# RWKV-7 inside a hybrid decoder step: even and odd heads on opposite partition halves, small products alternating between the two

## The chip, the cores and the metric

The kernel runs on one core of one Trainium2 chip. The metric is the device time of one execution in microseconds (us). All arithmetic that matters is in 32-bit floats: the large projections split each operand into two fp32r parts and make three products of them, the small recurrent products use plain f32. In the trace a plain f32 product of two operands appears as two weight loads and two matmul records; a transpose appears as one. Counts of records below are counts in the trace, not of calls in the code.

## The reference, cut to what matters

One layer runs RWKV-7 heads and HGRN2 heads side by side from one input projection, joins them in one output projection, and follows with a squared-ReLU MLP. It does so for a prompt of 1024 tokens and for 8 decode sequences of 4 tokens ("samples"). Only the RWKV part is touched:

```python
def step(s, inp):
    r_t, w_t, k_t, v_t, kk_t, a_t = inp
    sa = jnp.einsum('bhvk,bhk->bhv', s, -kk_t)
    s = (s * w_t[:, :, None, :] + sa[..., None] * (kk_t * a_t)[:, :, None, :]
         + v_t[..., None] * k_t[:, :, None, :])
    o = jnp.einsum('bhvk,bhk->bhv', s, r_t)
    return s, o
```

There are 8 heads of width 64. The kernel doesn't step through tokens. It takes chunks of 64 tokens, builds for each head the 64x64 matrices that say how tokens of the chunk act on each other, inverts one triangular matrix per head, and carries a 64x64 state per head from chunk to chunk.

## The kernel before, in words

The program has two halves. The first, the **mixers**, computes the input projection, the RWKV and HGRN2 recurrences and the conditioning (`ada_pair`); the second does the output projection and the MLP with a Strassen-like scheme (`out_project`, `up`, `down`, products on line 1137) and isn't touched. In the mixers three generators are emitted in turn: the main one (projections `ps_in`, lines 208 to 210, and HGRN2), `ada`, and `rwkv`. Their yields set the order in which work is emitted; a list scheduler then orders each engine's queue at build time, and every engine runs its queue in that order.

RWKV takes the prompt in 8 groups of 128 tokens (2 chunks each) and one group for the samples (1 chunk). A group passes through these stages, and three groups are in flight at a time:

- `rwkv_prep` loads the projected rows as 4 tiles (index j) of 128 partitions. Partitions 0 to 63 of tile j hold one head (h = 0, even), 64 to 127 the next (h = 1, odd). The low-rank products `ps_lora` (line 695) use rows 0 to 63 of a weight for the decay and rows 64 to 127 for the gate `a`. Line 747 and 749 write `bb` and `kd` into the tile `bk`. `ps_v` (line 769) transposes v into token-major form, 4 transposes a group, and line 772 copies it to `R`.
- `rwkv_attn`: `ps_A` (line 793), per chunk and head half 4 products of 64 rows and 128 columns; two VectorE multiplications by a mask (line 795) give `Aa` and `Ar`. Then `ps_bt` (line 809) and `ps_W` (line 815): per chunk 8 products with 64 rows, 64 columns, 64 moving columns. All of one chunk's `ps_W` read one half of the partitions and write the other: which half is set by the chunk's parity, not by the head.
- `rwkv_inv`, on GpSimd, inverts 32x32 blocks that travel through DRAM (`at_d`, `xt_d`); `rwkv_inv2` joins them with three rounds of small products (`ps_x0`, `ps_x1`, `ps_x2`: lines 896, 900, 904), 8 products of 32x32 a round and chunk, each round followed by a copy on ScalarE that the next round needs. One chunk's products all lie at one partition offset.
- `rwkv_chain` carries the state: `ps_U` (line 928) for h = 0, a VectorE add (line 929), `ps_U` for h = 1, another add, `ps_SA` (line 933), a copy (line 934) into `R`, `ps_S` (line 940), the new state (lines 946, 947), and `ps_O` (lines 953 and 954), where for each j and h a 64x64 product of `ar` with the state is followed by a product of `Ar` with `R` over all 128 rows, into the same place. `rwkv_centre` evacuates `ps_O`.
- `rwkv_finish` normalises and writes the output rows.

`ps_S` has a form worth knowing: over all 128 rows, it writes for each j first output partitions 0 to 63 (h = 0), then 64 to 127 (h = 1).

PSUM for RWKV consists of four single-buffered tags, `PT = "maso"`: one bank each for `rwkv_prep` ("m"), `rwkv_attn` and `rwkv_inv2` ("a"), `ps_U`, `ps_SA` and `ps_S` ("s"), and `ps_O` and the output transposes ("o").

Of the kernel before, what the change touches and what calls it, by code (L numbers as in the profile page):

```python
# [7 lines left out]
F32 = mybir.dt.float32  # L8
# [6 lines left out]
P = 128  # L15
# [51 lines left out]
B_Aa = 4  # L67
# [52 lines left out]
LEVELS = [1, 2, 4, 8, 16, 32, 64]  # L120

# [34 lines left out]
class Kernel:  # L156
# [511 lines left out]
    def rwkv_prep(self, g, pool, pp, x_d):  # L668
# [3 lines left out]
        c0, n, nch, sample = g["c0"], g["n"], g["nch"], g["sample"]  # L672
        X = pool.tile([P, 14, n], F32, tag="X", name="X", bufs=B_X)
# [18 lines left out]
        for li, dst, bias in ((slice(0, 64), sg, self.hw0), (slice(64, 128), a, self.ha0)):  # L692
            ps = pp.tile([P, 4, n], F32, tag=PT[0], name="ps_lora")
            for j in range(4):
                nc.tensor.matmul(ps[:, j, :], lhsT=self.lora[li, 0, j * P:(j + 1) * P], rhs=X[li, 12, :], start=True, stop=True)
            for j in range(4):
# [15 lines left out]
        g["bk"] = bk = pool.tile([P, 4, nch, P], F32, tag="bk", name="bk", bufs=B_bk)  # L712
        bx = bk.rearrange("p j c (s t) -> p j (c s) t", t=64)
        bb, kd = bx[:, :, 1:1 + nch, :], bx[:, :, 0::3, :] if nch == 2 else bx[:, :, 0:1, :]
        S.activation(rd, ch(cs), AF.Exp, scale=-DECAY0)
        S.activation(kd, ch(cs), AF.Exp, scale=DECAY0)
        S.activation(al, ch(sg), AF.Exp, scale=-DECAY0)
        g["pt"] = pt = pool.tile([P, 4, NS if sample else nch], F32, tag="pt", name="pt", bufs=B_pt)
# [10 lines left out]
        G.tensor_tensor(ch(a), ch(a), kd, op=ALU.mult)  # L729
# [37 lines left out]
        ps = pp.tile([n, 4, P], F32, tag=PT[0], name="ps_v")  # L767
        for j in range(4):
            nc.tensor.transpose(ps[:, j, :], v[:, j, :], self.ident)
        for e in range(nch):  # L770
            hs = slice(e * 64, (e + 1) * 64)
            S.activation(R[e].rearrange("p j h v -> p (j h v)")[hs, :], ps[hs].rearrange("p j x -> p (j x)"), AF.Copy)
        yield

    def rwkv_attn(self, g, pool, pp):
# [4 lines left out]
        g["Aa"], g["Ar"], g["bt_"] = [], [], []  # L780
        mask = self.amask_s if sample else self.amask
        nhf = 1 if sample else 2
        ni = nch * nhf * 8
# [1085 lines left out]
```

## Time and profile before

| what | us |
|---|---|
| runs shown, median of 3 (lowest to highest) | 1934.76 (1928.95 to 1952.22) |
| the profiled execution, its own time | 1959.38 |
| its span in the trace | 1957.6 |
| TensorE matmul busy | 1793.7 (92% of the span) |
| VectorE / ScalarE / GpSimd busy | 1175.9 / 919.0 / 994.3 |

The profiled execution is 1.3% slower than the median of the runs. A busy matmul engine in these profiles counts each record from start to its modelled end, so neighbours overlap: whether products follow each other densely is read from start to next start in the timeline, or by comparing groups that move the same number of columns. The granted clock is a share of 2.4 GHz; it is either 1 or one half at any moment, so a mean of 0.83 over a stretch means that a third of the stretch ran at 1.2 GHz.

### The profile page before, as it was taken

To read this page: it belongs to the slowest core of one execution; us is meant where nothing else is said; L and a number is where in the kernel's file an instruction comes from. 1 tells how busy PE (TensorE), PEld (TensorE's weight loads), DVE (VectorE), ACT (ScalarE), POOL (GpSimd) and SP (SyncE) were. 2 spreads that over 40 slices of the span, in tenths; PEclk is the share of its full clock that TensorE was granted. 3 is DMA by queue.
4 is the path that set the end of the run, shared out by engine and by line. 5 is a ranking of instruction groups with operands and counts; after the bars stand their busy time and mean duration, and the time that the engine had idled before them with its cause. 6 is when DMAs were issued, how large, how long until landed. Compare 5 with 4: busy or idle time off the path is not lost. (4 is left out here: it accounts for less than half of the span.)

```text
span 1957.6 us, 38042 instructions
## 1 busy us (share of the span) xinstructions
PE 1793.7 (92%) x13988; PEld 1646.0 (84%) x13988; DVE 1175.9 (60%) x2286; ACT 919.0 (47%) x1915; POOL 994.3 (51%) x1418
## 2 busy tenths in 40 slices
PE   6889889899899999999999799699999999999795
PEld 3778778767788888888888799699999899999795
DVE  7676834534744534565544456853333768799998
ACT  5455343653534455555463454545455454333332
POOL 4766362363617233336263566764544637264564
PEclk9998899867679878888796899899999999999896
DMA  7876578645558775635352743353333431423022
GB/s 264 280 235 192 174 237 262 196 125 138 146 154 262 232 230 157 195 117 175 114 160 64 250 170 104 107 167 117 98 99 125 145 132 53 136 75 127 19 76 89
DMA packets 219593, 303.33 MB, mean 155 GB/s; under 512 B 48616, under 2 KB 111464, under 8 KB 216336
## 3 DMA queue, kind: packets, MB, share of 16 engines
q1 hardware_dynamic: 199232, 275.74, 44.6%
q10 hardware_dynamic: 20080, 25.11, 3.8%
q8 instruction: 110, 1.80, 0.4%
q14 instruction: 75, 0.61, 0.1%
q0 software_dynamic: 96, 0.07, 0.0%
HBM read 237.17 MB, written 61.44 MB: 153 GB/s over the span
## 5 line engine op out<-in xcount | busy, mean ns | idle before, releaser
L1137 PE MATMUL ps_g<-bh,whi 128*128 128x264 f32 x1792 | 377.6, 291 | 51.1 <-DVE acc L1449 15.6
L1137 PE MATMUL ps_g<-bh,wlo 128*128 128x264 f32 x1792 | 374.3, 290 | 3.2 <-DVE wlo L1126 3.2
L1137 PE MATMUL ps_g<-bl,whi 128*128 128x264 f32 x1792 | 376.3, 290 | 0.7 <-DVE bl L1426 0.6
L1137 PEld LDWEIGHTS ps_g<-bh,whi 128*128 128x128 f32 x1792 | 287.7, 193 | 55.2 <-ACT whi L1125 16.3
L210 PE MATMUL ps_in<-h,wlo 128*128 128x256 f32 (+1 forms) x960 | 299.0, 313 | 10.0 <-POOL wlo L199 5.6
L208 PE MATMUL ps_in<-h,whi 128*128 128x256 f32 (+1 forms) x960 | 301.1, 318 | 5.7 <-ACT h L1090 3.5
L209 PE MATMUL ps_in<-l,whi 128*128 128x256 f32 (+1 forms) x960 | 298.3, 311 | 3.4 <-DVE l L1091 3.3
L1137 PEld LDWEIGHTS ps_g<-bh,wlo 128*128 128x128 f32 x1792 | 286.0, 193 | 3.8 <-DVE wlo L1126 3.8
L1137 PEld LDWEIGHTS ps_g<-bl,whi 128*128 128x128 f32 x1792 | 287.4, 194 | 1.3 <-DVE bl L1426 1.3
L195 ACT ACTIVATE whi<-wraw 128x512 fp32r<-128x512 f32 x240 | 149.5, 628 | 183.3 <-PE ps_in L209 122.4
L210 PEld LDWEIGHTS ps_in<-h,wlo 128*128 128x128 f32 x960 | 200.1, 209 | 23.1 <-POOL wlo L199 7.9
L208 PEld LDWEIGHTS ps_in<-h,whi 128*128 128x128 f32 x960 | 200.0, 210 | 14.7 <-issue 4.6
L209 PEld LDWEIGHTS ps_in<-l,whi 128*128 128x128 f32 x960 | 200.9, 209 | 10.1 <-DVE l L1091 4.3
L1125 ACT ACTIVATE whi<-wd 128x512 fp32r<-128x512 f32 x112 | 70.1, 630 | 184.2 <-PE ps_g L1137 152.8
L238 POOL TENSOR_TENSOR walo<-wada,wahi 128x256 fp32r<-128x256 f32 x128 | 95.9, 762 | 97.6 <-ACT wahi L237 88.3
L1126 POOL TENSOR_TENSOR wlo<-wu,whi 128x512 fp32r<-128x512 f32 x64 | 90.2, 1412 | 83.4 <-ACT whi L1125 83.2
L1125 ACT ACTIVATE whi<-wu 128x512 fp32r<-128x512 f32 x112 | 69.3, 628 | 119.6 <-PE ps_g L1137 111.0
L1426 POOL TENSOR_TENSOR bl<-u,bh 128x528 fp32r<-128x528 f32 x34 | 63.1, 1862 | 87.9 <-ACT bh L1425 77.8
L862 POOL TENSOR_TENSOR itmp<-ixt,iat 128x60 f32<-128x60 f32 (+24 forms) x248 | 76.1, 307 | 36.0 <-DMA iat<-at_d 17.6
L1426 DVE TENSOR_TENSOR bl<-u,bh 128x528 fp32r<-128x528 f32 x78 | 88.5, 1163 | 5.4 <-ACT bh L1425 5.3
L1126 DVE TENSOR_TENSOR wlo<-wd,whi 128x512 fp32r<-128x512 f32 x91 | 82.7, 913 | 12.3 <-ACT whi L1125 12.3
L864 POOL TENSOR_TENSOR ixt<-ixt,itmp 128x60 f32<-128x60 f32 (+24 forms) x248 | 78.1, 315 | 15.3
(426 smaller groups left out, 3910.7 us busy)
## 6 DMA issues: line engine op xcount, KB each, us to landing
wraw<-w_in SPq DMA_DIRECT2D x240, 256.0 KB, 4.1
wlo<-wlo_d SPq DMA_DIRECT2D x180, 256.0 KB, 3.9
wu<-w_up SPq DMA_DIRECT2D x74, 256.0 KB, 3.0
u<-u_d SPq DMA_DIRECT2D x16, 1056.0 KB, 4.9
wada<-w_ada SPq DMA_DIRECT2D x64, 256.0 KB, 3.8
wd<-w_down SPq DMA_DIRECT2D x64, 256.0 KB, 2.7
wlo_d<-wlo SPq DMA_DIRECT2D x60, 256.0 KB, 3.3
u_d<-c SPq DMA_DIRECT2D x48, 264.0 KB, 3.4
```

The source lines that it names most:

```text
L195: nc.scalar.activation(hi, raw, AF.Copy)
L208: nc.tensor.matmul(out, lhsT=wh, rhs=ah, start=first and k == 0, stop=False)
L209: nc.tensor.matmul(out, lhsT=wh, rhs=al, start=False, stop=False)
L210: nc.tensor.matmul(out, lhsT=wl, rhs=ah, start=False, stop=last and k == len(w) - 1)
L238: (nc.vector if k in ADV else nc.gpsimd).tensor_tensor(lo, raw[:, :, k, :], hi.bitcast(F32), op=ALU.subtract)
L862: G.tensor_tensor(tm, xt[:, 0:ns, j:j + 1].to_broadcast([P, ns, w]), at[:, j, j + 1:32].unsqueeze(1).to_broadcast([P, ns, w]), op=ALU.mult)
L864: G.tensor_tensor(dst, dst, tm, op=ALU.add)
L1125: self.nc.scalar.activation(hi, src, AF.Copy)
L1126: eng.tensor_tensor(lo, src, hi.bitcast(F32), op=ALU.subtract)
L1137: nc.tensor.matmul(out[c], lhsT=w[x][:, k, :], rhs=a[y][:, k, c * 264:c * 264 + 264], start=first and k == 0 and j == 0, stop=last and k = ...
L1426: F().tensor_tensor(lo[:, k, :], src[:, k, :], hi[:, k, :].bitcast(F32), op=ALU.subtract)
```

## The change

The token-side operands are laid out by head parity instead of chunk parity: within `bk`, `Aa`, `W`, `U`, `XT` and `R`, the even heads' part lies on one half of the partitions and the odd heads' on the other, for every chunk. Each group of small products then loops over j outside and the two halves inside, so that consecutive products lie on different partition halves of the operands (and, but for `ps_A` and `ps_lora`, of the output). `ps_lora` and `ps_A` use two PSUM tags ("m" and "a") at a time, one for each half. `ps_O` is split: its 8 products with the state come first, in a burst of their own ahead of `ps_SA`; its 8 products with `R` follow `ps_S`. `ps_U` is one burst with one add of 128 partitions. `rwkv_inv2` does both chunks of a group in each round. `ps_v` becomes products with a 64x64 piece of the identity. The two writes into `bk` become four half-width ones, the `R` copies two half-width ones.

```diff
-        for li, dst, bias in ((slice(0, 64), sg, self.hw0), (slice(64, 128), a, self.ha0)):
-            ps = pp.tile([P, 4, n], F32, tag=PT[0], name="ps_lora")
-            for j in range(4):
+        pl = [pp.tile([P, 4, n], F32, tag=PT[i], name="ps_lora") for i in range(2)]
+        for j in range(4):
+            for li, ps in zip(HALVES, pl):
                 nc.tensor.matmul(ps[:, j, :], lhsT=self.lora[li, 0, j * P:(j + 1) * P], rhs=X[li, 12, :], start=True, stop=True)
...
-        V.tensor_tensor(bb, ch(kk), ch(a), op=ALU.mult)
         V.tensor_tensor(rd, ch(r), rd, op=ALU.mult)
-        V.tensor_tensor(kd, ch(k), kd, op=ALU.mult)
+        for h, hs in enumerate(HALVES):
+            V.tensor_tensor(bk[hs, :, :, 1 - h, :], ch(kk[hs]), ch(a[hs]), op=ALU.mult)
+            V.tensor_tensor(bk[hs, :, :, h, :], ch(k[hs]), ch(sg[hs]), op=ALU.mult)
...
-        for j in range(4):
-            nc.tensor.transpose(ps[:, j, :], v[:, j, :], self.ident)
+        ps = pp.tile([P, nch, 4, 64], F32, tag=PT[0], name="ps_v")
         for e in range(nch):
-            hs = slice(e * 64, (e + 1) * 64)
-            S.activation(R[e].rearrange("p j h v -> p (j h v)")[hs, :], ps[hs].rearrange("p j x -> p (j x)"), AF.Copy)
+            for j in range(4):
+                for hs in HALVES:
+                    nc.tensor.matmul(ps[hs, e, j, :], lhsT=v[hs, j, e * 64:(e + 1) * 64], rhs=self.ident[hs, hs], start=True, stop=True)
+        for e in range(nch):
+            for h, hs in enumerate(HALVES):
+                S.activation(R[e][hs, :, h, :], ps[hs, e], AF.Copy)
...
+            pa = [pp.tile([P, 4, P], F32, tag=PT[h], name="ps_A") for h in range(2)]
+            for j in range(4):
+                for hs, ps in zip(HALVES, pa):
+                    nc.tensor.matmul(ps[:, j, :], lhsT=bk[hs, j, c].rearrange("p s t -> p (s t)"), rhs=ar[hs, j, c, :, :], start=True, stop=True)
...
+        ps = pp.tile([P, nch, 4, 64], F32, tag=PT[1], name="ps_W")
+        for c in range(nch):
+            for j in range(4):
+                for h, hs in enumerate(HALVES):
+                    nc.tensor.matmul(ps[HALVES[1 - h], c, j, :], lhsT=Aa[hs, h, c, j, :], rhs=R[c][hs, j, h, :], start=True, stop=True)
+        g["W"] = W = pool.tile([P, nch, 4, 64], F32, tag="W", name="W", bufs=B_W)
+        S.activation(W, ps, AF.Copy)
...
+        ps = pp.tile([P, n, 32], F32, tag=PT[1], name="ps_x1")
+        for i in range(n):
+            for h, (lo, hi) in enumerate(zip(los, his)):
+                nc.tensor.matmul(ps[hi, i, :], lhsT=g["Aa"][lo, h, i // 4, i % 4, 32:64], rhs=x11[lo, i, :], start=True, stop=True)
+        for hi in his:
             S.activation(t1[hi], ps[hi], AF.Copy)
...
+                U = pool.tile([P, 4, 64], F32, tag="U", name="U", bufs=B_U)
+                ps = pp.tile([P, 4, 64], F32, tag=PT[2], name="ps_U")
                 for j in range(4):
+                    for h, hs in enumerate(HALVES):
+                        nc.tensor.matmul(ps[HALVES[1 - h], j, :], lhsT=ar[hs, j, c, 0, :], rhs=st[hs, j, :], start=True, stop=True)
+                V.tensor_tensor(U, ps, W[:, c], op=ALU.add)
+
+            po = pp.tile([P, 4, 64], F32, tag=PT[3], name="ps_O")
+            if st is not None:
+                for j in range(4):
+                    for hs in HALVES:
+                        nc.tensor.matmul(po[hs, j, :], lhsT=ar[hs, j, c, 1, :], rhs=st[hs, j, :], start=j == 0, stop=False, skip_group_check=True)
+            ps = pp.tile([P, 4, 64], F32, tag=PT[2], name="ps_SA")
+            for j in range(4):
+                for bs in HALVES[::-1]:
+                    nc.tensor.matmul(ps[bs, j, :], lhsT=XT[bs, c, j, :], rhs=U[bs, j, :], start=True, stop=True)
+            for h, bs in enumerate(HALVES[::-1]):
+                S.activation(R[bs, :, h, :], ps[bs], AF.Copy)
             yield
...
             for j in range(4):
-                for h in range(2):
-                    hs = slice(h * 64, h * 64 + 64)
-                    if st is not None:
-                        nc.tensor.matmul(ps[hs, j, :], lhsT=ar[hs, j, c, 1, :], rhs=st[hs, j, :], start=True, stop=False)
-                    nc.tensor.matmul(ps[hs, j, :], lhsT=Ar[:, h, j, :], rhs=R[:, j, h, :], start=st is None, stop=True)
-            self.rwkv_centre(pool, g, c, ps)
+                for h, hs in enumerate(HALVES):
+                    nc.tensor.matmul(po[hs, j, :], lhsT=Ar[:, h, j, :], rhs=R[:, j, h, :], start=st is None and j == 0, stop=j == 3, skip_group_check=True)
+            self.rwkv_centre(pool, g, c, po)
```

The sample group is treated alike (`ps_Us` and `ps_SAs` alternate between two 32-partition places). `at_d` and `xt_d` are written and read by head parity instead of by chunk, with the same number of transfers for a prompt group and one more each for the sample group.

## Rows read from the trace of the kernel before

**Rows 1.** Windows: stretch, its us, PE, PEld, DVE, ACT, POOL busy, clock, DMA, GB/s.
```profile
100.00:1086.00 986.00, 926.14 (x7346) 804.76 (x7344) 513.86 (x1390) 481.52 (x1130) 449.72 (x1001) 0.83 0.58 177
1086.00:1958.00 872.00, 792.56 (x6244) 785.51 (x6244) 593.02 (x756) 387.20 (x673) 484.41 (x316) 0.94 0.35 116
1026.00:1062.00 36.00, 36.00 (x275) 29.53 (x274) 14.52 (x46) 12.86 (x33) 13.62 (x22) 0.52 0.23 65
```
**Rows 2.** Waits of the matmul engine from 100 to 1090 us, longest first.
```profile
PE ps_ada L246 <- ACT adt L243: 9.9, 3, 6.5
PE ps_hy L514 <- ACT ho L510: 5.2, 3, 3.8
```
**Rows 3.** Matmul groups by line and form: name, shape, xrecords, busy us, mean ns, idle before.
```profile
L793 PE MATMUL ps_A<-ar,bk 64*128 64x128 f32 x272 | 48.2, 320 | 0.0
L954 PE MATMUL ps_O<-R,Ar 128*64 128x64 f32 x256 | 42.3, 257 | 0.0
L953 PE MATMUL ps_O<-st,ar 64*64 64x64 f32 x240 | 42.0, 259 | 0.9 <-DVE hss L508 0.9
L928 PE MATMUL ps_U<-st,ar 64*64 64x64 f32 x240 | 26.5, 265 | 0.0
L695 PE MATMUL ps_lora<-X,lora 64*128 64x128 f32 x128 | 22.4, 324 | 1.9 <-ACT X L680 1.9
L815 PE MATMUL ps_W<-R,Aa 64*64 64x64 f32 x272 | 21.2, 233 | 2.3 <-ACT btm L811 2.3
L933 PE MATMUL ps_SA<-U,XT 64*64 64x64 f32 x240 | 21.0, 250 | 0.0
L896 PE MATMUL ps_x<-ident,XT 32*32 32x32 f32 x256 | 13.6, 211 | 3.2 <-ACT W L818 3.2
L940 PE MATMUL ps_S<-R,btm 128*64 128x64 f32 x256 | 12.1, 240 | 0.0
L995 PE MATMUL ps_Us<-st_s,ax 64*32 64x64 f32 x128 | 7.5, 216 | 0.0
L769 PE MATMUL ps_v<-ident,X 128*128 128x128 f32 x32 | 5.6, 303 | 0.0
```
**Rows 4.** Windows as rows 1, of ps_O alone: PE, PEld, ACT busy.
```profile
100.00:1086.00 986.00, 70.23 (x496) 50.40 (x496) 6.12 (x16) 0.83 0.58 177
```
**Rows 5.** Timeline of the matmul engine: start, us, line, names, shape, xrecords.
```profile
1014.56 0.69 PE L896 MATMUL ps_x<-ident,XT 32*32 32x32 f32 x16
1015.18 1.14 PE L933 MATMUL ps_SA<-U,XT 64*64 64x64 f32 x16
1016.25 0.49 PE L497 MATMUL ps_o<-hst,hqe 128*128 128x128 f32 x2
...
1019.26 0.69 PE L940 MATMUL ps_S<-R,btm 128*64 128x64 f32 x16
1019.78 0.28 PE L954 MATMUL ps_O<-R,Ar 128*64 128x64 f32 x2
1019.99 0.33 PE L953 MATMUL ps_O<-st,ar 64*64 64x64 f32 x2
1020.24 0.33 PE L954 MATMUL ps_O<-R,Ar 128*64 128x64 f32 x2
1020.50 0.33 PE L953 MATMUL ps_O<-st,ar 64*64 64x64 f32 x2
```
**Rows 6.** Groups on VectorE and ScalarE, 100 to 1090 us, columns as rows 3.
```profile
L929 DVE TENSOR_TENSOR U<-ps_U,W 64x256 f32<-64x256 f32 x30 | 12.6, 421 | 30.9 <-PE ps_U L928 30.6
L747 DVE TENSOR_TENSOR bk<-kk,a 128x512 f32<-128x512 f32 x8 | 5.6, 699 | 0.0
L818 ACT ACTIVATE W<-ps_W 64x512 f32<-64x512 f32 x17 | 10.0, 591 | 12.0 <-PE ps_W L815 8.8 <-PE ps_in L209 3.2
L897 ACT ACTIVATE x<-ps_x 32x256 f32<-32x256 f32 x16 | 5.9, 372 | 14.6 <-PE ps_x L896 14.5
```

More of the change, by code (lines that the diff above doesn't have):

```diff
@@ L66 @@
 B_R = 4
-B_Aa = 4
+B_Aa = 2
 B_Ar = 4
@@ L120 @@
 LEVELS = [1, 2, 4, 8, 16, 32, 64]
+HALVES = (slice(0, 64), slice(64, 128))
 VEC = {}
@@ L728, in rwkv_prep @@
         G.tensor_tensor(k, k, cs, op=ALU.mult)
-        G.tensor_tensor(ch(a), ch(a), kd, op=ALU.mult)
+        G.tensor_tensor(a, a, sg, op=ALU.mult)
         sq = cs
@@ L788, in rwkv_attn @@
             Ar = pool.tile([P, 2, 4, 64], F32, tag="Ar", name="Ar", bufs=B_Ar)
-            for h in range(2):
-                hs = slice(h * 64, h * 64 + 64)
-                ps = pp.tile([P, 4, P], F32, tag=PT[1], name="ps_A")
-                for j in range(4):
-                    nc.tensor.matmul(ps[:, j, :], lhsT=bk[hs, j, c, :], rhs=ar[hs, j, c, :, :], start=True, stop=True)
-                for dst, o in ((Aa, 0), (Ar, 64)):
-                    V.tensor_tensor(dst[:, h], ps[:, :, o:o + 64], mask[:, o:o + 64].unsqueeze(1).to_broadcast([P, 4, 64]), op=ALU.mult)
@@ L803, in rwkv_attn @@
+            for h, ps in enumerate(pa):
+                for dst, o in ((Aa[:, h, c], 0), (Ar[:, h], 64)):
+                    V.tensor_tensor(dst, ps[:, :, o:o + 64], mask[:, o:o + 64].unsqueeze(1).to_broadcast([P, 4, 64]), op=ALU.mult)
             g["Ar"].append(Ar)
             yield
+        for h in range(2):
+            for hf in range(nhf):
+                p0 = 64 * (1 - h) + hf * 32
+                i0 = (hf * 2 + h) * nch * 4
+                nc.sync.dma_start(
+                    g["at_d"][i0:i0 + nch * 4].rearrange("i s t -> s i t"),
+                    Aa[p0:p0 + 32, h, :, :, hf * 32:hf * 32 + 32].rearrange("s c j t -> s (c j) t"))
@@ new lines, in rwkv_inv2 @@
+        n = nch * 4
+        x11 = pool.tile([P, n, 32], F32, tag="x11", name="x11", bufs=B_x11)
+        t1 = pool.tile([P, n, 32], F32, tag="xt1", name="xt1", bufs=B_xt1)
+        los = [slice(64 * (1 - h), 64 * (1 - h) + 32) for h in range(2)]
+        his = [slice(64 * (1 - h) + 32, 64 * (1 - h) + 64) for h in range(2)]
+        for hi in his:
+            G.memset(XTi[hi, :, 0:32], 0.0)
+        ps = pp.tile([P, n, 32], F32, tag=PT[1], name="ps_x0")
+        for i in range(n):
+            for lo in los:
+                nc.tensor.matmul(ps[lo, i, :], lhsT=XTi[lo, i, 0:32], rhs=self.ident[lo, lo], start=True, stop=True)
@@ new lines, in rwkv_inv2 @@
+        for lo in los:
+            S.activation(x11[lo], ps[lo], AF.Copy)
+        yield
+        ps = pp.tile([P, n, 32], F32, tag=PT[1], name="ps_x1")
+        for i in range(n):
+            for h, (lo, hi) in enumerate(zip(los, his)):
+                nc.tensor.matmul(ps[hi, i, :], lhsT=g["Aa"][lo, h, i // 4, i % 4, 32:64], rhs=x11[lo, i, :], start=True, stop=True)
+        for hi in his:
+            S.activation(t1[hi], ps[hi], AF.Copy)
+        yield
+        ps = pp.tile([P, n, 32], F32, tag=PT[1], name="ps_x2")
@@ L908, in rwkv_chain @@
+        for i in range(n):
+            for lo, hi in zip(los, his):
+                nc.tensor.matmul(ps[lo, i, :], lhsT=t1[hi, i, :], rhs=XTi[hi, i, 32:64], start=True, stop=True)
+        for lo in los:
+            S.activation(XTi[lo, :, 32:64], ps[lo], AF.Copy)
+        yield
     def rwkv_chain(self, g, pool, pp):
@@ L937, in rwkv_chain @@
             for j in range(4):
-                for h in range(2):
-                    hs = slice(h * 64, h * 64 + 64)
+                for h, hs in enumerate(HALVES):
                     nc.tensor.matmul(ps[hs, j, :], lhsT=bt[:, j, hs], rhs=R[:, j, h, :], start=True, stop=True)
```

112 lines of the change are left out of this document (31 added, 81 removed).

## The prediction

> **What bounds the kernel now.** I read the windows view first, since the change touches only the mixers. From 100 to 1086 us the matmul engine is busy 926.1 of 986 us, while VectorE, ScalarE and GpSimd are busy 514, 482 and 450 us and the DMA engines 58% of the time; the granted clock is 0.83 there, against 0.94 in the half of the program that isn't touched [rows 1]. Then the waits of the matmul engine: its longest source, the small conditioning product behind a copy on ScalarE, sums to 9.9 us and the next to 5.2 us [rows 2]. So nothing else holds the mixers: what ends last there is TensorE's own queue. "Busy" counts each record to its modelled end, though, so I went on to the groups by form [rows 3] and the timeline [rows 5] to see how densely the small products follow each other. The reader should see three things.
>
> First, `ps_SA`: 16 records of 64x64 on one partition half, started at 1015.18, and the next product starts at 1016.25: 67 ns a record. Second, `ps_S`: 16 records with the same 64 moving columns, but consecutive products write opposite halves of the output: 1019.26 to 1019.78, 33 ns a record [rows 5]. Over all chunks the same contrast stands in the groups: `ps_SA` 21.0 us / 240 = 87.5 ns a record, `ps_S` 12.1 us / 256 = 47.3 ns, a ratio of 0.54 [rows 3]. Both belong to the same chunk steps, so both carry about the same mixture of the two clock levels. Third, `ps_O`, where a 64x64 product and a 128x64 product take turns: each start is 0.25 to 0.26 us after the last [rows 5], where a product of `ps_SA` (two records) takes 1.07 / 8 = 0.134 us. A change of the shape costs about 0.12 us, and there are 248 products in that alternation: 70.2 us together [rows 4].
>
> **The change, part by part.** The yardstick for a product that alternates halves is `ps_S`, 47.3 ns a record or 0.54 of the time it takes now.
>
> - `ps_O`: 70.2 us now [rows 4]. Afterwards 240 records of the state product in bursts (240 x 47.3 ns = 11.4 us) and 256 records over all rows, written to alternating halves exactly like `ps_S` (12.1 us). Saved: 46.7 us. This is the largest term, and about half of it needs no overlap at all, only that the shapes no longer alternate.
> - `ps_U`: 26.5 to 11.4 us, saved 15.1. `ps_SA`: 21.0 to 11.4, saved 9.6. `ps_W`: 21.2 to 272 x 47.3 ns = 12.9, saved 8.3. The three rounds of `ps_x`, of which the row of one is shown: 3 x 13.6 = 40.8, times 0.54 = 22.0, saved 18.8. `ps_Us`: 7.5 to 4.1, saved 3.4 [rows 3].
> - `ps_A` and `ps_lora` alternate the operand's half alone, and both halves write all 128 output partitions, into two banks. The trace has no such pair. Bounds: nothing saved (they queue as now), or 0.54 as for `ps_S`. I take 0.54, since in `ps_S` too it is that the second product uses the other half of the array that lets it start early. Saved: 48.2 - 26.0 = 22.2 and 22.4 - 12.1 = 10.3 us [rows 3].
> - `ps_v`: 32 records for the 8 prompt groups take 5.6 us now [rows 3]; afterwards 16 products a group, 2 records each, 256 records: 12.1 us. Lost: 6.5.
>
> Sum: 46.7 + 15.1 + 9.6 + 8.3 + 18.8 + 3.4 + 22.2 + 10.3 - 6.5 = 127.9 us. Busy time of a burst runs about 0.07 us past the next start (1.14 us against 1.07 [rows 5]); there will be some 72 fewer bursts (15 of `ps_U`, 8 of `ps_W`, 24 of `ps_x`, 17 of `ps_A`, 8 of `ps_lora`) and 15 more of `ps_O`, so 57 x 0.07 = 4 us of that was never on the path. 124 us remain.
>
> Other engines. VectorE: the two writes into `bk` become four; if a half-width one costs as much as the full one (699 ns), that is 2 x 9 x 0.699 = 12.6 us more, if it costs half, nothing; the 30 adds of `ps_U` become 15, 15 x 0.421 = 6.3 us less [rows 6]. So between -6.3 and +6.3 us on an engine that idles for 472 us of the stretch [rows 1]: hidden by TensorE's work, at most 6.3 us if that cover were gone. ScalarE: 33 copies into `R` of about 591 ns (the nearest row, `W`) become 66 of about 372 ns (the nearest narrow one, `ps_x`): +5.1 us; copies of `W` go from 17 to 9: -4.7 us [rows 6]; nil. GpSimd clears the same areas. DMA: the same number of transfers for a prompt group and two more of some 16 KB in the whole program, on SP's queue, ahead of which nothing new waits; nil.
>
> Waits and order. `ps_A` now needs two banks, "m" and "a", free at once; "m" was last used by `ps_v` of the same group, evacuated by then. In exchange it doesn't wait between its halves for its own bank. The early part of `ps_O` holds bank "o" from before `ps_SA`, and so must wait until the copy of the previous chunk's `ps_O` is done; that copy follows directly on the previous burst, several other products earlier in TensorE's queue. If it were late, the queue behind it, projections included, would stand for one copy (0.59 us by the nearest row, that of `W` [rows 6]), times 15: 9 us. The chain itself gets shorter: one add instead of product, add, product, add before `ps_SA`; three rounds of copies per group in `rwkv_inv2` instead of six. The only longer path is that the transfer of chunk 0's `Aa` to DRAM waits for chunk 1's: GpSimd picks it up a stage later anyhow.
>
> Of the 124 us I carry 94% to the end, the share of the stretch in which TensorE is busy now (926 / 986 [rows 1]): 117 us. The profiled execution took 1959.4 us, so 1842 us on its terms. It lies 1.3% above the median of the runs shown; scaled by 1934.76 / 1959.38 the forecast is **1819 us**.
>
> **The rivals.**
>
> *The halves don't overlap when they write one bank.* In `ps_S` both products read all rows and differ in output partitions only. In `ps_U`, `ps_SA`, `ps_W`, `ps_x`, `ps_v` and the state part of `ps_O` the operands' rows differ too, and both write one bank. No row shows such a pair back to back with its like. If they go one after another, these keep 87.5 ns a record: `ps_O` 70.2 - 21.0 - 12.1 = 37.1 saved, `ps_A` and `ps_lora` 32.5 saved, `ps_v` 256 x 87.5 ns - 5.6 = 16.8 lost, the others nil: 53 us, times 0.94 = 50: 1909, scaled 1885 us. For it: nothing in the rows excludes it. Against: their output partitions are as disjoint as those of `ps_S`. The Trainium skill's "TensorEngine Tiling (Array Packing)", section "Restrictions and Gotchas", says that different row tiles cannot access the same PSUM bank at the same time; by that rule this rival is what happens, and no row of the trace before shows it either way. Chance 0.12.
>
> *The gain meets another limit.* With TensorE's load down by an eighth, the recurrences' chains of copies and adds might set the pace in places. If half is lost: 1959.4 - 62 = 1897, scaled 1874 us. Against it: none of the other engines is over 53% busy [rows 1]. Chance 0.14.
>
> *Slower: every change of half drains the array as a change of shape does.* Place: all bursts that now alternate, 136 + 64 + 120 + 120 + 136 + 384 + 128 + 64 = 1152 products (`ps_A`, `ps_lora`, `ps_U`, `ps_SA`, `ps_W`, `ps_x`, `ps_v`, `ps_Us`). At 0.12 us each, 138 us more, against 23 us saved on the part of `ps_O` over all rows (35.1 - 12.1): 2074, scaled 2048 us. It decides from 23 / 1152 = 0.02 us a change. Against: `ps_S` changes its output half at every product and pays nothing. For: no row shows a change of the operand's half within one shape. Chance 0.04.
>
> *The clock moves.* In the 36 us from 1026 on, full of thin bursts, the granted clock was 0.52 [rows 1]. Denser bursts may lift it: the mixers' remaining 869 us at 0.83 become 829 at 0.87, a gain of 40 us: 1802, scaled 1779 us, chance 0.10. If gaps take the place of the thin work and the clock falls to 0.76, the loss is 80 us: 1922, scaled 1898 us, chance 0.05.
>
> **How the numbers follow.** The forecast has the remaining chance, 0.55, with a range of its own of 1780 to 1850 us: 32.5 x 0.94 = 31 us upwards if `ps_A` and `ps_lora` save nothing, the clock's gain downwards. The whole range, 1765 to 1890 us, takes in the clock's gain with some room, the half-lost gain and the one-bank case, and leaves out the drains, the falling clock and the tails. Two per cent, about what a measurement of this kernel can tell from no change, is 1896 us: all cases but the drains and the falling clock lie below, some of the half-lost and one-bank ones only just. Faster 0.88, within 2% 0.08, slower 0.04.
>
> **What the profile after would show.** Right: `ps_U`, `ps_SA`, `ps_W` near 47 ns a record instead of 80 to 110; `ps_O` near 24 us in two groups; `ps_A` near 26 us; the mixers ending near 970 us; the second half unchanged at 872 us. Wrong: bursts of 16 still taking 1.07 us from start to next start (one bank); over 0.2 us a product (drains); bursts short but the mixers still past 1020 us, with new waits of the matmul engine beyond the present 60 us (another limit); a granted clock in the mixers outside 0.80 to 0.87.

## The result, and the profile after

The changed kernel takes 1863.49 us (median of 4, 1859.36 to 1870.08) beside 1940.3 us for the kernel before on the same chip (median of 4): a ratio of 0.9607, 95% interval 0.9537 to 0.9677. It is faster by 77 us, 4%, where 6% was forecast; 1863 lies inside the whole range (1765 to 1890), and outside the likeliest case's own range (1780 to 1850). The profiled execution took 1859.36 us, its span is 1857.6 us.

The windows view after, columns as in [rows 1]:

```profile
100.00:1086.00 986.00, 874.54 (x8266) 771.54 (x8266) 574.25 (x1485) 527.54 (x1237) 522.94 (x1048) 0.89 0.64 197
100.00:1000.00 900.00, 789.19 (x7579) 686.60 (x7578) 527.30 (x1399) 485.33 (x1166) 468.14 (x1009) 0.88 0.64 197
1000.00:1858.00 858.00, 788.47 (x6242) 781.51 (x6242) 589.41 (x748) 381.13 (x661) 472.83 (x308) 0.95 0.34 115
950.00:1001.00 51.00, 18.05 (x259) 15.33 (x259) 8.37 (x28) 11.95 (x26) 22.42 (x52) 0.51 0.28 86
```

The granted clock in 100 to 1086 us is 0.89 instead of 0.83; the last 86 us of that stretch now belong to the part behind the mixers, and up to 1000 us alone it is 0.88. The mixers (all that lies ahead of the first `ps_g` product on `yh`) now end at 1000.4 us instead of 1095.1; what follows takes 857 us (862.5 before, and 857 to 864 in all the runs below). The last row has no counterpart before: in the last 51 us of the mixers TensorE is busy for 18 us, at a clock of 0.51.

The small products, grouped by line and form, columns as in [rows 3]:

```profile
L794 PE MATMUL ps_A<-ar,bk 64*128 64x128 f32 x272 | 46.0, 315 | 4.5 <-ACT R L776 2.0 <-DVE bk L751 1.8 <-DVE Ar L797 0.6
L697 PE MATMUL ps_lora<-X,lora 64*128 64x128 f32 x128 | 21.0, 320 | 0.9 <-DVE Ar L797 0.9
L963 PE MATMUL ps_O<-R,Ar 128*64 128x64 f32 x256 | 17.9, 244 | 0.9 <-ACT R L948 0.9
L946 PE MATMUL ps_SA<-U,XT 64*64 64x64 f32 x240 | 14.9, 258 | 0.6 <-ACT XT L915 0.5 <-DVE U L936 0.2
L942 PE MATMUL ps_O<-st,ar 64*64 64x64 f32 x240 | 14.3, 246 | 0.6 <-DVE bot L1057 0.6
L953 PE MATMUL ps_S<-R,btm 128*64 128x64 f32 x256 | 13.9, 246 | 0.0
L935 PE MATMUL ps_U<-st,ar 64*64 64x64 f32 x240 | 13.0, 245 | 2.1 <-DVE st L960 1.3 <-DVE mod L248 0.7
L773 PE MATMUL ps_v<-ident,X 64*64 64x64 f32 x272 | 11.4, 238 | 2.2 <-DVE kk L759 2.2
L819 PE MATMUL ps_W<-R,Aa 64*64 64x64 f32 x272 | 10.8, 234 | 3.8 <-ACT btm L812 3.8
L899 PE MATMUL ps_x<-ident,XT 32*32 32x32 f32 x256 | 7.1, 211 | 24.2 <-DMA XT<-xt_d 24.2
```

Against [rows 3], `ps_U`, `ps_W` and this round of `ps_x` are halved, `ps_SA` is down by 6 us and `ps_O` fell from 42.3 + 42.0 to 17.9 + 14.3. `ps_A` and `ps_lora` hardly moved, and `ps_x` has 24.2 us of idle time ahead of it where it had 3.2.

For a ledger I split the length of the mixers in the trace into three parts: TensorE's idle time, its busy time counted as if all of it ran at full clock, and what the half clock adds (half of the busy time spent at 1.2 GHz instead of 2.4). Before: 92.7 + 840.0 + 162.5 = 1095 us. After: 136.1 + 774.5 + 89.7 = 1000 us. So 65 us of work went, the half clock cost 73 us less, and 43 us of idle time came back; with 5 us behind the mixers that is the 100 us between the two profiled executions. Some executions fall into a slower state, over 1.5% longer at a lower clock; they are left out of the medians here, but the profiled one of the kernel before is one of them (mean clock 0.887, where the median of the 26 others listed with the runs below is 0.90), so the 73 us are too many. By 2 x (1 - clock) x span, the median execution spends 382 us at half clock before and 309 us after (0.917). By medians the clock is therefore worth about (382 - 309) / 2 = 36 us of the 77, an estimate that takes TensorE to be busy in that time.

### The profile page after: what moved, and what is told of

Read it like the earlier page. It is cut to its first block, busy times and chain, and to the rows that moved or that the text cites. A ratio compares the mean times of both kernels' runs of the same rounds, so it can differ in the third digit from the quotient of the medians.

```text
span 1857.6 us, 38545 instructions
## 1 busy us (share of the span) xinstructions
PE 1652.4 (89%) x14224; PEld 1523.4 (82%) x14224; DVE 1186.8 (64%) x2289; ACT 918.1 (49%) x1943; POOL 1002.9 (54%) x1419
## 5 line engine op out<-in xcount | busy, mean ns | idle before, releaser
L1147 PE MATMUL ps_g<-bh,whi 128*128 128x264 f32 x1792 | 375.6, 290 | 50.4 <-DVE acc L1459 14.2
L211 PE MATMUL ps_in<-h,wlo 128*128 128x256 f32 (+1 forms) x960 | 290.6, 305 | 8.4 <-POOL wlo L200 5.5
L209 PE MATMUL ps_in<-h,whi 128*128 128x256 f32 (+1 forms) x960 | 290.0, 306 | 8.9 <-DVE mod L248 3.3
L210 PE MATMUL ps_in<-l,whi 128*128 128x256 f32 (+1 forms) x960 | 286.8, 300 | 3.6 <-DVE l L1101 3.6
L211 PEld LDWEIGHTS ps_in<-h,wlo 128*128 128x128 f32 x960 | 190.3, 199 | 19.8 <-POOL wlo L200 7.6
L209 PEld LDWEIGHTS ps_in<-h,whi 128*128 128x128 f32 x960 | 190.1, 200 | 17.1 <-ACT h L1100 4.4
L210 PEld LDWEIGHTS ps_in<-l,whi 128*128 128x128 f32 x960 | 191.3, 199 | 8.4 <-DVE l L1101 4.5
L864 POOL TENSOR_TENSOR itmp<-ixt,iat 128x60 f32<-128x60 f32 (+24 forms) x248 | 83.3, 336 | 46.4 <-DMA iat<-at_d 32.0
```

The source lines that it names most:

```text
L209: nc.tensor.matmul(out, lhsT=wh, rhs=ah, start=first and k == 0, stop=False)
L210: nc.tensor.matmul(out, lhsT=wh, rhs=al, start=False, stop=False)
L211: nc.tensor.matmul(out, lhsT=wl, rhs=ah, start=False, stop=last and k == len(w) - 1)
L864: G.tensor_tensor(tm, xt[:, 0:ns, j:j + 1].to_broadcast([P, ns, w]), at[:, j, j + 1:32].unsqueeze(1).to_broadcast([P, ns, w]), op=ALU.mult)
L1147: nc.tensor.matmul(out[c], lhsT=w[x][:, k, :], rhs=a[y][:, k, c * 264:c * 264 + 264], start=first and k == 0 and j == 0, stop=last and k = ...
```

## The experiments

The ledger for every run, in us: the median time, the time at half clock in the median execution (2 x (1 - clock) x span), and three numbers from the mixers of the profiled one. e6 was run once.

| kernel | time | at half clock | work at full clock | idle | mixers end |
|---|---|---|---|---|---|
| before | 1940.3 | 382 | 840.0 | 92.7 | 1095.1 |
| after | 1863.5 | 309 | 774.5 | 136.1 | 1000.4 |
| e1, halves in turn | 1898.9 | 357 | 803.6 | 115.1 | 1036.1 |
| e2, only `ps_O` split | 1876.8 | 328 | 814.0 | 95.5 | 1016.5 |
| e12, `ps_O` interleaved | 1890.8 | 348 | 807.9 | 126.0 | 1043.3 |
| e4, `ps_A`, `ps_lora` in turn | 1867.4 | 321 | 773.7 | 135.1 | 1003.3 |
| e5, their halves, diagonal | 1891.7 | 353 | 773.6 | 143.7 | 1020.7 |
| e6, their halves, rows first | 1861.7 | 290 | 782.5 | 139.7 | 998.8 |
| e3, last inversion on VectorE | 1860.2 | 327 | 775.0 | 122.5 | 1001.6 |
| e8, RWKV paced x 1.08 | 1860.2 | 296 | 776.9 | 131.4 | 993.1 |
| e9, RWKV early in one pass | 1867.9 | 319 | 780.8 | 124.7 | 1002.6 |
| e13, RWKV paced x 1.16 | 1859.7 | 327 | 774.9 | 125.0 | 998.1 |
| e14, 25 yields | 1861.2 | 307 | 777.8 | 132.8 | 997.7 |
| e15, e14 and e3 | 1856.5 | 306 | 777.7 | 121.2 | 991.1 |

### Which part of the change brings the time?

e1 keeps the new layout and the split `ps_O`, and takes the alternation of halves away, in all tiles but `ps_A` and `ps_lora`, which e4 looks at (the part of `ps_O` on `R` is left as it is too; shown is the loop of `ps_U`):

```diff
-                for j in range(4):
-                    for h, hs in enumerate(HALVES):
+                for h, hs in enumerate(HALVES):
+                    for j in range(4):
                         nc.tensor.matmul(ps[HALVES[1 - h], j, :], lhsT=ar[hs, j, c, 0, :], rhs=st[hs, j, :], start=True, stop=True)
```

> The changed kernel with its layout, its split ps_O and its merged bursts, but in every burst whose operands and outputs both change halves (ps_U, ps_SA, ps_W, the three ps_x, ps_v, the state part of ps_O, ps_Us) all products of one half come first, then all of the other. Theory (alternation itself lets two products overlap): ps_W, ps_U, ps_SA go back to 58 ns from start to start at full clock, about 85 ns a record over the run, ps_v to 22 us; some 60 us of matmul time come back, of which the time shows about 50: 1910 us. Rival (the gain came from fewer and longer bursts, shorter chains and the split of ps_O): within 10 us of the changed kernel, 1855 to 1875 us.

Measured: 1898.86 us, ratio to before 0.9782 (0.9716 to 0.9848). That is 35 us above the changed kernel, between the two forecasts: the alternation alone carries 35 us of the gain, less than the theory's 50. From its groups view:

```profile
L935 PE MATMUL ps_U<-st,ar 64*64 64x64 f32 x240 | 19.4, 254 | 2.1 <-DVE st L960 2.1
L946 PE MATMUL ps_SA<-U,XT 64*64 64x64 f32 x240 | 20.3, 263 | 0.5 <-ACT XT L915 0.5
L819 PE MATMUL ps_W<-R,Aa 64*64 64x64 f32 x272 | 15.5, 241 | 2.1 <-ACT btm L812 2.1
```

The same records in the same layout take 19.4, 20.3 and 15.5 us where alternating they take 13.0, 14.9 and 10.8.

e2 is the other way round: the kernel before, with only the part of `ps_O` on the state pulled out into a burst of its own ahead of `ps_SA`.

```diff
+            if st is not None:
+                for j in range(4):
+                    for h in range(2):
+                        hs = slice(h * 64, h * 64 + 64)
+                        nc.tensor.matmul(po[hs, j, :], lhsT=ar[hs, j, c, 1, :], rhs=st[hs, j, :], start=j == 0, stop=False, skip_group_check=True)
...
-                    if st is not None:
-                        nc.tensor.matmul(ps[hs, j, :], lhsT=ar[hs, j, c, 1, :], rhs=st[hs, j, :], start=True, stop=False)
```

> The kernel before, with one edit: the 8 products of ps_O with the state are issued in a burst ahead of ps_SA, the 8 with R in a burst after ps_S; layout and all other bursts as before. Theory (a change of shape between neighbours costs 0.12 us, and in bursts the halves alternate): ps_O falls from 70 to between 24 and 35 us, and the time by 30 to 45 us, to about 1900 us. Rival (the chain of copies and adds sets the pace around ps_O, so that its burst time doesn't count): ps_O shorter, but the time within 10 us of 1940 us.

Measured: 1876.75 us, 0.965 (0.9572 to 0.9727), more than either theory allowed. Its groups and its window:

```profile
L935 PE MATMUL ps_O<-st,ar 64*64 64x64 f32 x240 | 15.6, 246 | 2.9 <-DVE bot L1050 2.9
L957 PE MATMUL ps_O<-R,Ar 128*64 128x64 f32 x256 | 14.2, 252 | 0.0
```

```profile
100.00:1086.00 986.00, 910.69 (x7889) 803.62 (x7888) 550.66 (x1469) 520.02 (x1193) 496.69 (x1037) 0.89 0.63 196
```

`ps_O` falls to 15.6 + 14.2 us, and the clock in the stretch rises to the 0.89 that the whole change has. Part of this 0.89 is the part behind the mixers, which begins at 1016.5 here. In the median execution 54 us less are spent at half clock than before, worth 27 of the 63 us gained.

e12 completes the square: the changed kernel with `ps_O` interleaved again.

```diff
-            if st is not None:
-                for j in range(4):
-                    for hs in HALVES:
-                        nc.tensor.matmul(po[hs, j, :], lhsT=ar[hs, j, c, 1, :], rhs=st[hs, j, :], start=j == 0, stop=False, skip_group_check=True)
...
-                    nc.tensor.matmul(po[hs, j, :], lhsT=Ar[:, h, j, :], rhs=R[:, j, h, :], start=st is None and j == 0, stop=j == 3, skip_group_check=True)
+                    if st is not None:
+                        nc.tensor.matmul(po[hs, j, :], lhsT=ar[hs, j, c, 1, :], rhs=st[hs, j, :], start=True, stop=False)
+                    nc.tensor.matmul(po[hs, j, :], lhsT=Ar[:, h, j, :], rhs=R[:, j, h, :], start=st is None, stop=True)
```

> The changed kernel with ps_O's two products a head in turn again, as the kernel before has them (state product, then intra-chunk product, head by head); all else of the change stays. Theory A (the change of shape inside ps_O, 107 to 152 ns a record in the kernel before, costs its own time and also the clock: ps_O held TensorE most just ahead of 10 of the 27 falls of the clock there, and of none where ps_O alone was split): about 40 us of TensorE time at full clock come back and the time at half clock in the mixers rises from 231 us towards 300 or more; a part is absorbed by the idle time that the changed kernel has more (128 against 85 us): 1900 to 1925 us. Theory B (the clock gain of the run with ps_O alone split was luck of the order): only ps_O's own time comes back, less the idle time, half-clock time stays under 250 us: about 1880 us.

Measured: 1890.81 us, 0.9817 (0.9718 to 0.9917). Its groups and its window:

```profile
L961 PE MATMUL ps_O<-R,Ar 128*64 128x64 f32 x256 | 46.6, 277 | 0.9 <-ACT R L943 0.9
L960 PE MATMUL ps_O<-st,ar 64*64 64x64 f32 x240 | 45.6, 278 | 1.6 <-DVE bot L1055 1.6
```

```profile
100.00:1086.00 986.00, 884.11 (x7902) 767.75 (x7902) 553.65 (x1441) 505.53 (x1200) 498.50 (x1030) 0.87 0.62 192
```

`ps_O` is back at 92 us busy, and 27 us of the time come back by the medians, about 40 by the ratios. Half-clock time rises by 39 us (in e1 by 48); in the profiled mixers it is 273 us, where theory A had 300 or more and B under 250. The time lies between the two forecasts as well (1900 to 1925, and 1880).

Of the 27 falls of the clock in the mixers of the kernel before, 10 came when `ps_O` had held TensorE most just ahead of them (some 150 of the 355 us at half clock); in e2 it was none of 24, but with the same interleaved `ps_O`, in e12, at most 1 of 21. So theory A's reason for the clock, that the changes of shape inside `ps_O` bring it down, isn't borne out.

The two products that take turns in `ps_O` differ in shape, but they also add into the same place, which could be what costs. The trace before tells the two apart. At full clock the first record of the product with `R` starts 148 ns after the last of the state product, and the next state product 151 to 152 ns after the last record of that one, where records of one shape on one half follow at 58 ns. From `ps_U` (64x64) to the projections `ps_in`, which write elsewhere, it is 148 to 149 ns too, and from `ps_O`'s 128x64 products to them 151 to 152. It is the change of shape.

What follows from the four corners, by the ratios and in us of 1940: splitting `ps_O` alone gains 68 us, the rest of the change alone about 36, both 76, some 27 us less than the sum of the two. The intervals of the three ratios together are about as wide as that, so the times alone make the shortfall likely and don't show it. The ledger points the same way: the work saved more than adds up (26.0 and 32.1 us at full clock, together 65.5), the idle time doesn't (95.5 us in e2, 126.0 in e12, 136.1 in the changed kernel).

e1 and e2, measured on one chip, say where that comes from. e1 has e2's split and the new layout and staging besides, without alternation, and it is 22 us slower: 10 us less work, but 20 us more idle time and 29 us more at half clock (some 5 us of busy time are the state part of `ps_O`, which alternates in e2 alone). So the new layout and staging without the alternation cost time, and the alternation has to earn that back first.

### Why did `ps_A` and `ps_lora` save nothing?

e4 takes their alternation away:

```diff
-            for j in range(4):
-                for hs, ps in zip(HALVES, pa):
+            for hs, ps in zip(HALVES, pa):
+                for j in range(4):
```

> The changed kernel, but ps_A and ps_lora issue all products of one operand half, then all of the other (both halves write all 128 output partitions). Theory (halves of the operand alone don't overlap, as 46 us of ps_A in the changed kernel against 48 us before suggest): 112 ns from start to start in both, time within 4 us of 1863 us. Rival, the step of the prediction (they overlap, but something else lengthened them): 20 to 30 us slower.

Measured: 1867.35 us, 0.9613 (0.955 to 0.9677): no difference. `ps_A` takes 45.9 us instead of 46.0:

```profile
L794 PE MATMUL ps_A<-ar,bk 64*128 64x128 f32 x272 | 45.9, 314 | 3.5 <-DVE bk L751 1.9 <-ACT R L776 0.9 <-DVE Ar L797 0.7
```

Alternating or not, the next record starts 112 ns after the last at full clock. e5 cuts each of these products into two of 64 output columns (64 partitions of the result) and orders them so that neighbours differ in operand half and in output half (shown for `ps_A`):

```diff
-                for hs, ps in zip(HALVES, pa):
-                    nc.tensor.matmul(ps[:, j, :], lhsT=bk[hs, j, c].rearrange("p s t -> p (s t)"), rhs=ar[hs, j, c, :, :], start=True, stop=True)
+                for h, o in ((0, 0), (1, 1), (0, 1), (1, 0)):
+                    hs = HALVES[h]
+                    nc.tensor.matmul(pa[h][HALVES[o], j, :], lhsT=bk[hs, j, c, o, :], rhs=ar[hs, j, c, :, :], start=True, stop=True)
```

> The changed kernel with each ps_A and ps_lora product cut into two of 64 output columns (800 records instead of 400), issued so that consecutive ones differ in operand half and in output half. Theory A (two products overlap where both their rows and their columns differ, as ps_U, ps_W and ps_O did; ps_A failed because its products take all 128 columns): about 40 ns a record at full clock, so ps_A's 272 products fall from 46 to about 33 us and ps_lora's from 21 to about 15; with the waits behind them 5 to 15 us faster than the changed kernel, about 1853 us. Theory B (ps_A is bound by something else, as its operand loads, that the cut doubles): 80 ns a record or more, 30 us slower.

e6 has the same pieces in the order `((0, 0), (1, 0), (0, 1), (1, 1))`, so that within a pair only the operand's half differs:

> The same cut products of ps_A and ps_lora in another order: consecutive ones differ in operand half alone within a pair (same output columns), and in both between pairs. Theory A (a difference in rows alone gives no overlap): two kinds of start to start, about 58 ns or more inside a pair, well under 40 ns between pairs; ps_A's sum above that of the order with both halves changing by 5 us or more. Theory B (the cut alone makes the overlap): the same sum as in the other order.

Measured: e5 1891.72 us, 0.9761 (0.9694 to 0.9828); e6 1861.66 us in one execution. One burst each, from the timelines of the matmul engine at full clock (start, us, line, names, shape, records), first after, then e6:

```profile
376.57 1.16 PE L794 MATMUL ps_A<-ar,bk 64*128 64x128 f32 x8
```

```profile
370.53 1.09 PE L796 MATMUL ps_A<-ar,bk 64*64 64x128 f32 x16
```

Eight records of whole products take 1.16 us, sixteen of halves 1.09: hardly any work is saved. Start to start, at full clock, the pieces follow at 7, 103, 7, 103 ns in both orders, so two of them do run side by side, in e6 also where both write the same 64 columns and differ in rows alone. But the pair takes 110 ns, as long as one record of a whole product. My 40 ns a record was wrong: it came from products with 64 moving columns, whose pair takes 7 + 52 = 59 ns, and `ps_A` moves 128. No more than two do: the next pair, which needs the same two row halves, starts when this one is through, in either order. Of e6's theories B holds (about the same sum: 42.9 us, and 40.6 in e5, over all 544 records, start to start). Of e5's neither does: the pieces overlap as A said, but at 55 ns a record and without a gain; the time is B's, without B's 80 ns. That e5 is 28 us slower than the changed kernel at the same work goes mostly with its clock: 353 us at half clock in the median execution instead of 309, worth 22 us. Why this order has it and that of e6 (290, in its one execution) doesn't, no run here tells.

### Why is TensorE idle at the end of the mixers?

In the timeline of the matmul engine after, and of GpSimd (the last two rows), columns as in [rows 5], idle time and its cause in brackets:

```profile
953.29 1.02 PE L247 MATMUL ps_ada<-two,adt 18*128 18x9 f32 x4
977.78 0.31 PE L899 MATMUL ps_x<-ident,XT 32*32 32x32 f32 x2 [23.48 <-DMA XT<-xt_d]
...
957.15 1.26 POOL L1136 TENSOR_TENSOR wlo<-wo,whi 128x512 fp32r<-128x512 f32 x1
...
971.69 0.21 POOL L866 TENSOR_TENSOR ixt<-ixt,itmp 128x8 f32<-128x8 f32 x1
```

The conditioning product at 953.29 is the last of the main work. Then TensorE waits 23.48 us for the last RWKV group, whose block inversion on GpSimd ends at 971.9, among weight splits for the next part. In the kernel before the inversion ended at 1027.9 us, with main work on TensorE until about 1085:

```profile
1027.71 0.21 POOL L864 TENSOR_TENSOR ixt<-ixt,itmp 128x8 f32<-128x8 f32 x1
```

e3 moves the last group's inversion to VectorE:

```diff
-                G.tensor_tensor(tm, xt[:, 0:ns, j:j + 1].to_broadcast([P, ns, w]),
+                E = V if g["c0"] == SC + TP - GN else G
+                E.tensor_tensor(tm, xt[:, 0:ns, j:j + 1].to_broadcast([P, ns, w]),
...
-                G.tensor_tensor(dst, dst, tm, op=ALU.add)
+                E.tensor_tensor(dst, dst, tm, op=ALU.add)
```

> The changed kernel, but the multiplications and additions of the block inversion of the last RWKV group run on VectorE instead of GpSimd; the other seven groups are as they were. Theory (the 23.5 us for which TensorE stands before ps_x near 954 us is the wait for GpSimd's inversion of the last group): that wait shrinks to under 10 us and the time falls by 12 to 20 us, to about 1848 us. Rival (TensorE would have waited there for something else, the transfers through DRAM or the chain before it): the wait moves, and the time stays within 5 us of 1863 us.

Measured: 1860.18 us, 0.9574 (0.9512 to 0.9637).

```profile
979.06 1.46 PE L900 MATMUL ps_x<-ident,XT 32*32 32x32 f32 x32 [7.73 <-DMA XT<-xt_d]
...
968.64 0.17 DVE L867 TENSOR_TENSOR ixt<-ixt,itmp 128x8 f32<-128x8 f32 x1
```

The wait falls to 7.7 us, as the theory had it, but the inversion ends only 3 us earlier, since on VectorE it queues in order behind other work. And `ps_x` starts no earlier: from the end of the inversion to it, the way through DRAM, now takes 10.3 us instead of 5.9, with loads of the next weights (`wo`) issued between its two legs on SyncE. TensorE's other work now runs up to 971 us instead of 954. The time is the rival's.

A prompt group of RWKV yields 27 times in the changed kernel and 25 times before, so at unchanged pacing factors (`RS0` to `RS7`) it is emitted later against the main work. e8 and e13 multiply all factors, e9 raises one, e14 takes the two yields out:

```diff
-RS6 = 0.85
+RS6 = 1.15
```

```diff
         S.activation(W, ps, AF.Copy)
-        yield
...
             S.activation(t1[hi], ps[hi], AF.Copy)
-        yield
```

> The changed kernel with all RWKV pacing factors times 1.08, that is 27/25: its RWKV helper now yields 27 times a prompt group where the kernel before yielded 25, so at the same factors it is emitted later against the rest. Theory A (TensorE's 23.5 us idle time before the last ps_x at 977.78 us is bought by this later emission): the wait shrinks to under 10 us and the time is 10 to 20 us lower, about 1848 us. Theory B (the last group's inversion is late for another cause, or an earlier inversion only moves the idle time to another place of the in-order queues): the time stays within 6 us of the changed kernel.

> The changed kernel with one pacing factor raised, 0.85 to 1.15: RWKV's work is emitted faster during the second-to-last pass of the main work (HGRN2), nothing else differs. Theory A (the last group is late against the main work): its inversion ends while main work still runs, the 23.5 us wait before ps_x goes, about 1845 us. Theory B (what is pulled forward waits in the in-order queues of its own stage, or the chain of the last group is the limit whatever is emitted when): within 6 us of the changed kernel, or slower.

> The changed kernel with all RWKV pacing factors times 1.16 (times 1.08 gave 1860 us, with the wait before the last ps_x cut from 23.5 to 10.6 us and 122 us of TensorE idle time in the mixers instead of 128). Theory A (the end wait is pure loss): the wait is gone and the time is another 5 to 10 us lower, about 1853 us. Theory B (the idle time is that of a section whose chains and other engines now bound it as much as TensorE; it only changes place): the time stays between 1856 and 1868 us, with 115 to 130 us of idle time in the mixers.

> The changed kernel with the two yields a prompt group that the change added taken out again (25 as before, not 27), pacing factors unchanged. Theory A (the two further yields made the last group late): the wait before the last ps_x falls to about 10 us, as with the pacing factors times 1.08, and the time is 0 to 5 us below the changed kernel. Theory B (lateness comes from main work that ends earlier now, whatever the count of yields): the wait stays above 18 us, the same time.

Measured: e8 1860.18 us, 0.9595 (0.9538 to 0.9651); e9 1867.88, 0.9636 (0.958 to 0.9691); e13 1859.68, 0.9612 (0.9527 to 0.9696); e14 1861.23, 0.9636 (0.9573 to 0.9698). In e8 the wait before `ps_x` is 10.6 us, in e9 6.1. The same row of the waits view (us in all, times, longest) of the changed kernel, of e12, of e13 and of e14:

```profile
PE ps_x L899 <- DMA XT<-xt_d: 24.2, 2, 23.5
```

```profile
PE ps_x L899 <- DMA XT<-xt_d: 20.0, 2, 19.2
```

```profile
PE ps_x L899 <- DMA XT<-xt_d: 10.4, 2, 10.1
```

```profile
PE ps_x L898 <- DMA XT<-xt_d: 9.2, 2, 8.9
```

The wait comes with the new staging, not with a faster TensorE: e1 (20.2 us) and e12 have it too, e2, with the old staging and the mixers 79 us shorter than before, doesn't. Taking the two yields out cuts it from 23.5 to 8.9 us. That much of the A theories holds. The price that e8, e9 and e13 put on it (5 to 20 us) doesn't: none of the four runs is more than 4 us below the changed kernel, whose own executions span 11 us, and e9 is 4 above. On e8, e9 and e13 the B theories were right about the time; on e14 theory A was right about the wait and, with 0 to 5 us, about the time.

e15 joins e14 and e3:

> The changed kernel with the two further yields taken out (alone: 1861 us, end wait 23.5 to 8.9 us) and the last group's block inversion on VectorE instead of GpSimd (alone: 1860 us, end wait 7.7 us). Theory A (the two cut the same wait from two sides and their remains add): no wait over 2 us before the last ps_x, the mixers end near 990 us, about 1850 us. Theory B (TensorE's idle time in the mixers is kept up by the section's chains, and what is taken at one place comes back at others, as in the four runs on pacing): the wait is gone, the idle time stays over 110 us, and the time is between 1855 and 1865 us.

Measured: 1856.54 us, 0.9618 (0.9576 to 0.9661). The wait is down to 3.5 us (timeline of the matmul engine, then the window at the end of the mixers):

```profile
953.75 0.31 PE L899 MATMUL ps_x<-ident,XT 32*32 32x32 f32 x2 [3.51 <-DMA XT<-xt_d]
```

```profile
950.00:1001.00 51.00, 36.59 (x426) 30.45 (x423) 20.54 (x64) 23.26 (x61) 26.07 (x29) 0.69 0.50 155
```

TensorE is busy for 36.6 of these 51 us, where it had 18 in the changed kernel; 9.0 of them belong to the part behind the mixers, which end 9 us earlier, at 991.1. Still 121 us of idle time remain, only 15 us less than in the changed kernel although 20 us of waiting are gone. The time is as theory B had it, and the mixers' end as A had it. Its ratio of 0.9618 against 0.9607 for the changed kernel doesn't show a version that beats it; directly the medians differ by 7 us, but the two were not run beside each other.

## Why the prediction was right or wrong

**The bound and the sign: right.** TensorE's queue held the mixers, and denser small products made the kernel faster. The two rivals on overlap fell. The bursts of `ps_U`, both halves writing one bank, run at 29 ns a record at full clock: 16 in 0.68 us, where the burst of `ps_SA` in [rows 5] took 1.14.

```profile
943.07 0.68 PE L935 MATMUL ps_U<-st,ar 64*64 64x64 f32 x16
```

Starts are 7 ns and then 52 ns apart: a pair of records on the two halves takes the time of one, and a change of half costs nothing that shows. The Trainium skill's "TensorEngine Tiling (Array Packing)", section "Restrictions and Gotchas", says that different row tiles cannot use one PSUM bank at the same time. By that rule the one-bank rival should have come true, and this trace disagrees, at least for products whose output partitions are disjoint.

**The terms of the sum.** By busy time, `ps_U`, `ps_SA` and `ps_W` together saved 13.5 + 6.1 + 10.4 = 30.0 us (33.0 forecast); the round of `ps_x` shown saved 6.5 us, which for three is 19.5 (18.8 forecast); `ps_Us` saved 3.1 (3.4 forecast); `ps_v` lost 4.8 (6.5 forecast), with the sample group in both sums. `ps_O` was mis-sized: 84.3 to 32.2 us by group; start to start (gaps counted up to 1 us) 67.7 to 27.9, so 40 us instead of 46.7. The yardstick was too good: the part that was to behave "exactly like `ps_S`" takes 17.9 us / 256 = 70 ns a record, and `ps_S` itself 54 instead of the 47.3 that I read. That `ps_S` and `ps_SA` "carry about the same mixture of the two clock levels" was wrong: before, 12% of `ps_S`'s records started at half clock and 32% of `ps_SA`'s; after, 19% of `ps_S`'s. With `ps_A` and `ps_lora`, below, the terms measure some 91 us of the 127.9, each kernel at its own mixture of clock levels; the ledger's 65 us are all at full clock.

**The step that failed: `ps_A` and `ps_lora`, 32.5 us.** I wrote the bounds, nothing or 0.54, and took 0.54 because `ps_S` overlaps in "the other half of the array". That was the wrong neighbour: the products of `ps_S` differ in output columns, those of `ps_A` in operand rows, with all 128 columns written. They saved 2.2 + 1.4 us, and e4 shows that this isn't the alternation's work. Times 0.94, and scaled, the missed 28.9 us are worth 27 us, where 44 lie between forecast and result.

**"94% carried": wrong in size, in both directions.** The idle time was to stay at 6% of the stretch. It rose by 43 us (92.7 to 136.1). Of that, 21 us are the wait before `ps_x`. Its larger cause isn't in the prediction at all: the change gives a group two more yields, and without them (e14) the wait is 8.9 us. Whether the clause that GpSimd picks the transferred `Aa` up "a stage later anyhow" fails for the last group, which has no main work behind it, and so accounts for the rest, no run tests. The 94% came from a stretch in which that work still covered the tail. The other half is spread over many short waits, and cutting the end wait in several ways (e3, e8, e9, e13, e14, e15) brought at most 7 us. So the "another limit" rival came true in part. Which chain sets the pace in the middle of the mixers isn't settled.

**The clock: the rival I gave 0.10 came true beside the forecast.** I had the mixers at 0.80 to 0.87; from 100 to 1000 us they ran at 0.88. By medians, 73 us less at half clock gave back some 36 us, most of what the idle time took. Both parts of the change lower the half-clock time: e2 has 54 us less of it than the kernel before, e12 has 34 less. What starts a fall stays open; e12 spoke against the interleaved `ps_O` as its cause.

**Other engines and waits: right in kind, VectorE's sum too small.** Each half-width write into `bk` costs as much as the full one did, or more (699 ns in [rows 6]):

```profile
L751 DVE TENSOR_TENSOR bk<-X,sg 64x512 f32<-64x512 f32 x16 | 14.0, 874 | 1.5 <-POOL X L729 1.4
L750 DVE TENSOR_TENSOR bk<-kk,a 64x512 f32<-64x512 f32 x16 | 11.7, 730 | 0.1
```

With the sample group the writes take 29.4 us instead of 11.9, and the adds of `ps_U` halve (15 at 411 ns), so VectorE has some 11 us more to do, where I had at most 6.3. TensorE's waits on the writes sum to 1.8 us (the row of `ps_A` above). The wait that I feared, of the early part of `ps_O` on bank "o", amounts to at most 0.6 us in all (the row of `ps_O<-st,ar` above).

In sum: 65 us of full-clock work saved, 36 us by the clock (medians) and 5 us of the part behind the mixers, less 43 us of new idle time, are 63 of the 77 us. The other 14 lie between a ledger of single executions and medians of many, and no run assigns them. The forecast of 117 us was all work; it was too high by the products that don't overlap, and the two things it held constant moved against each other by nearly the same amount. That is luck: without the clock's 36 us the time would have been near 1900 us, outside the whole range.

## What to carry to other kernels

Order small products so that neighbours use different halves both of operand rows and of output columns, and keep products of one shape together: here that halved the first kind, and the second was the largest single gain. Before counting an overlap for another pair, look for a row where neighbours differ in just the way that the new ones will, and compare equal moving widths. When a change adds a yield or a stage to one of several interleaved chains, look at the end of the section: the chain is emitted later against the others, and where the work that covered its tail has run out, the tail becomes a wait. And measure before mending it: here the wait shrank in six runs, and the time by 7 us at most.

## What the runs showed of the hardware that I had not expected

- Two f32 products of 64 operand rows and 64 output columns on different rows run side by side, two records at a time, whether their output columns differ (`ps_U`, e5) or not (e6, two banks); the pair takes 59 ns with 64 moving columns and 110 ns with 128. Two products of 64 rows that write all 128 columns don't: 112 ns a record at full clock, alternating or in turn (e4). The Trainium skill's "TensorEngine Tiling (Array Packing)", section "Key Properties", lets different tiles run in parallel; the trace agrees for two 64x64 tiles and not for 64x128.
- An interleaving of two shapes of product costs its own time, 74 us start to start in e12 against 28 us in bursts, for the same 496 records. At full clock, the first record after a change of shape starts 148 to 152 ns after a record with 64 moving columns (`ps_O`, `ps_U` to `ps_in`), instead of 58.
- The time at half clock can differ with the order of equal work: 353 us in e5 and 309 in the changed kernel, with 773.6 and 774.5 us of work at full clock. That is worth 22 us, 1.2% of the time.
